# Two changes to a diffusion trunk on one core: how modulation vectors are summed and spread, and how gathers are spaced over a loop

## The chip, the cores and the metric

One Trainium2 chip, one core, one launch. The metric is the time of the whole program on the device in microseconds (us). A kernel is run several times and its median is compared. Engines are named as in the profile: PE (matrix multiply) with PEld (its weight loads), DVE (vector), ACT (scalar), POOL, and SP, which here only issues transfers.

## The reference

A two-layer trunk over 256 latent and 256 context tokens of width 1024, in float32. Cut to what matters here:

```
for l in 0, 1:
    m  = silu(c)     @ ada_w[l] + ada_b[l]      # 6 vectors of 1024 for the latent tokens
    mc = silu(c_ctx) @ ada_w[l] + ada_b[l]      # the same for the context tokens
    sh1, sc1, g1, sh2, sc2, g2 = split(m)       # v = 0 .. 5 in the kernel
    h  = rmsnorm(x, norm1_g[l]) * (1 + sc1) + sh1
    y  = mixer(h, hc)                           # attention, a different one in each layer
    x  = x + g1 * y
    h2 = rmsnorm(x, norm2_g[l]) * (1 + sc2) + sh2
    x  = x + g2 * peer_ffn(h2)                  # sum over 16 of 16384 experts per head and token
    # context tokens likewise in layer 0 only (csh1 ... cg2 from mc)
out = rmsnorm(x, final_norm_g)
```

So each layer has six modulation vectors of 1024 numbers, twice (latent, context). Shifts and scales (v = 0, 1, 3, 4) are needed with the feature on the partition; gates (v = 2, 5) are needed as a row that is the same on all 128 partitions. `peer_ffn` multiplies every token with all 16384 rows of `peer_u`, weighs, and multiplies with all rows of `peer_v`; in layer 0 the fourth block of 128 tokens takes another way: it gathers, for each of its 128 (head, choice) pairs, one row of `peer_u` and one of `peer_v` per token by index.

## The kernel before

The program runs through fixed stages: a start (the first modulation vectors and the first norm), the mixer of layer 0, the expert stage of layer 0 (`peer(0, ...)`), the mixer of layer 1, the expert stage of layer 1, a last norm. Instructions of an engine run in one order that is fixed when the kernel is built; each waits for what it reads and for the buffer that it writes.

**Modulation.** `ada_mm(l, v, half, pool)` works out 512 columns of vector v for both token kinds. The left operand `cs` is silu(c) and silu(c_ctx), padded to 32 columns, as eight tiles of 128 inputs. The right operand comes in four tiles of 512 KB (`take(("ada", ...))`), each 128 output columns with all 1024 inputs. PE is used as four column groups of 32 (`tile_position=(0, 32 * j)`): group j sums input tiles 2j and 2j+1 for all 512 columns. So the result lies in PSUM as [128, 512]: four partial sums in rows 32j and 32j+1. A DVE add (L252) takes it out and adds the bias tile `bt`, which POOL has cleared (L238) and SP has loaded two rows into (L239).

`ada_end` adds up the four partial sums and brings them into their form. For shifts and scales four small matmuls with `rt` as stationary operand and the selector `sel` (128 x 2) give features on partitions (L270); a copy (L275) or a multiply with the norm's gain (L278) writes `self.mod`. For gates a matmul with the selector `selb` as stationary operand gives a [128, 512] tile with the row on all partitions (L261), once per token kind that the layer needs (two in layer 0, one in layer 1); ACT copies it out (L262), and SP stores its 256 KB in a DRAM tensor `gb` of 128 equal rows (L263). `out_proj` (L407) and `residual` (L1245) load 512 KB of it each, with

```
g = self.m.t("g4", [128, 1024], name="gb")
nc.sync.dma_start(g, self.gb[l, 0, s])
```

There are 24 halves (2 layers, 6 vectors, 2 halves): 16 of shifts and scales, 8 of gates. They are spread as a filler, a step at a time, between other work: `ada_first` at the start (v = 0, 1 of layer 0, 4 halves), `fill` in mixer0 (v = 2, 3, 4; 6 halves), `fill` in the prologue of `peer(0)` (v = 5 of layer 0, v = 0, 1 of layer 1; 6 halves), and `fill` in mixer1 (v = 2 to 5 of layer 1; 8 halves). `bt`, `ar` and `gbo` share the buffers "a2": 3 in mixer0, 2 in the prologue and in mixer1.

**Gathers.** The main loop of `peer(0)` has 128 iterations. Iteration j multiplies chunk j of `peer_v` (`fchunk`, 18 matmuls of 512 columns for three token blocks). While j + 27 < 128, it also multiplies chunk j + 27 of `peer_u` (`achunk`, 24 matmuls of 384 columns); so iterations 0 to 100 are long and 101 to 127 short. DVE, in its order, splits the next chunks into a rounded and a rest part (L169, with ACT's L168), makes the next weights (L1176, L1178), and then uses gathered tiles: n < 128 for the dot product with u (L1143), n from 128 to 255 for the sum over v (L1148). The gather of tile n + 5 is issued by POOL when tile n has been used, five buffers in all. How many are used in an iteration is said by `pace`, from iteration 12 to 124:

```
def at(i):
    return i + min(i, NCH - lag)
return min(256, -(-256 * (at(j + 1) - at(LATE)) // (at(NCH - 3) - at(LATE))))
```

Long iterations so count twice as much as short ones: 48 long ones use three tiles and 41 use two (226), of the short ones 6 use two and 18 one (30).

Of the kernel before, what the change touches and what calls it, by code (L numbers as in the profile page):

```python
# [10 lines left out]
F = mybir.dt.float32  # L11
# [5 lines left out]
OP = mybir.AluOpType  # L17
# [5 lines left out]
NCH = 128  # L23
EPS = 1e-6
NEG = -1e30
FMIN = -3e38
LAM_INIT = 0.8 - 0.6 * math.exp(-0.3)
MLA_SCALE = 96 ** -0.5
LAG = (27, 47)
LATE = 12  # L30
# [19 lines left out]
PK = {}  # L50
_o = 0
for _n, _w in (("n1_0", 8), ("n1_1", 8), ("n2_0", 8), ("n2_1", 8), ("qn", 2), ("kvn", 1), ("sub", 1),
               ("sink", 8), ("lam", 4), ("c", 16)):
    PK[_n] = (_o, _w)
    _o += _w
PK_W = _o
CK = {}
_o = 0
for _n, _w in (("ident", 128), ("iota", 128), ("lo", 16), ("sel", 2), ("selb", 256), ("r64", 128), ("r32", 128)):
    CK[_n] = (_o, _w)  # L60
    _o += _w
CK_W = _o
# [28 lines left out]
class Kernel:  # L91
# [141 lines left out]
    def ada_mm(self, l, v, half, pool):  # L233

        nc = self.nc
        n = 2 * v + half
        bt = pool.t("a2", [128, 512], name="bt")
        nc.gpsimd.memset(bt, 0.0)  # L238
        nc.sync.dma_start(bt[0:2, :], self.A["ada_b"][l, n * 512:n * 512 + 512].partition_broadcast(2))  # L239
        p = self.ps()  # L240
        for b in range(4):
            w = self.take(("ada", l, 4 * n + b), load=ADA_LOAD)
            for q in range(2):
                for j in range(4):
                    k = 2 * j + q
                    nc.tensor.matmul(p[32 * j:32 * j + 32, b * 128:(b + 1) * 128], self.cs[:, k, :],  # L246
                                     w[:, k * 128:(k + 1) * 128], start=(q == 0), stop=(q == 1),
                                     tile_position=(0, 32 * j))
            if b % 2:
                yield None  # L250
        rt = pool.t("a2", [128, 512], name="ar")
        nc.vector.tensor_tensor(rt, p, bt, op=OP.add)  # L252
        yield rt

    def ada_end(self, l, v, half, rt, pool):
        nc = self.nc
        if v in (2, 5):
            for s in range(2 if l == 0 else 1):
                g = pool.t("a2", [128, 512], name="gbo")
                p = self.ps()  # L260
                nc.tensor.matmul(p, self.ck("selb")[:, s * 128:(s + 1) * 128], rt, start=True, stop=True)  # L261
                nc.scalar.copy(g, p)  # L262
                nc.sync.dma_start(self.gb[l, v // 3, s][:, half * 512:half * 512 + 512], g)  # L263
                yield
            return
        if half == 0:
            self.mod[l, v] = self.const([128, 8, 2], name=f"mod{l}{v}")
        p = self.ps([128, 8])
        for k in range(4):
            nc.tensor.matmul(p[:, 2 * k:2 * k + 2], rt[:, k * 128:(k + 1) * 128], self.ck("sel"),  # L270
                             start=True, stop=True)
        oh = self.mod[l, v][:, half * 4:half * 4 + 4, :]
        ph = p.rearrange("p (k s) -> p k s", s=2)
        if v in (0, 3):
            nc.vector.tensor_copy(oh, ph)  # L275
        else:
            g = self.pk("n%d_%d" % (1 if v == 1 else 2, l))[:, half * 4:half * 4 + 4]
            nc.vector.scalar_tensor_tensor(oh, ph, 1.0, g[:, :, None].to_broadcast([128, 4, 2]), op0=OP.add,  # L278
                                           op1=OP.mult)
        yield  # L280

# [115 lines left out]
    def out_proj(self, l, yh, yl, src, T):  # L397
        nc = self.nc
        gs, xs = [], []
        sq = [self.small([128, 2], "sq") for _ in range(T)]  # L400
        for t in range(T):
            x = self.m.t("q4", [128, 1024], name="x")
            nc.sync.dma_start(x, src[t])
            xs.append(x)
        for s in range(T // 2):
            g = self.m.t("g4", [128, 1024], name="gb")
            nc.sync.dma_start(g, self.gb[l, 0, s])  # L407
            gs.append(g)
        rst = []
        for half in range(2):  # L410
            c = slice(half * 512, half * 512 + 512)
            ps = [self.ps() for _ in range(T)]

            def part(t, b, wh, wl):
                tt = slice(t * 128, (t + 1) * 128)
                for q in range(2):
                    wc = slice(q * 512, q * 512 + 512)
                    self.mm3(ps[t], yh[:, 2 * b + q, tt], yl[:, 2 * b + q, tt], wh[:, wc], wl[:, wc],
                             b == 0 and q == 0, b == 3 and q == 1)

            for b in range(2):
                w = self.take(("wout%d" % l, half * 4 + b))
                for t in range(T):
                    part(t, b, *w)
            w = [self.take(("wout%d" % l, half * 4 + b)) for b in (2, 3)]
            for t in range(T):
                for b in (2, 3):
                    part(t, b, *w[b - 2])
                tmp = self.m.t("h2", [128, 512], name="yt")
                nc.vector.tensor_tensor(tmp, ps[t], gs[t // 2][:, c], op=OP.mult)  # L430
                nc.vector.tensor_tensor(xs[t][:, c], xs[t][:, c], tmp, op=OP.add)
                rs = self.squares(xs[t], half, sq[t], ps[t])
                if half:
                    rst.append(rs)
        return xs, rst
# [555 lines left out]
    def peer(self, l, xs, sq, nd):  # L991
# [203 lines left out]
        def pace(j):  # L1195

            def at(i):
                return i + min(i, NCH - lag)
            return min(256, -(-256 * (at(j + 1) - at(LATE)) // (at(NCH - 3) - at(LATE))))

        nu = 0
        load_v(0)
# [28 lines left out]
    def residual(self, l, f):  # L1231

        nc = self.nc
        T = len(f)
        sq = [self.small([128, 2], "sq") for _ in range(T)]
        self.m = Phase(self.tc, "mix%d" % (l + 1), M_BUFS[1])
        xs = []
        for t in range(T):
            x = self.m.t("q4", [128, 1024], name="x")
            nc.sync.dma_start(x, self.xd[t])  # L1240
            xs.append(x)
        gs = []
        for s in range((T + 1) // 2):
            g = self.m.t("g4", [128, 1024], name="gb")
            nc.sync.dma_start(g, self.gb[l, 1, s])  # L1245
            gs.append(g)
        rst = [None] * T
        for t in (3, 0, 1, 2) if T == 4 else range(T):
            for half in range(2):
                b = slice(half * 512, half * 512 + 512)  # L1250
                tmp = self.m.t("h2", [128, 512], name="ft")
                nc.vector.tensor_tensor(tmp, f[t][half], gs[t // 2][:, b], op=OP.mult)
                nc.vector.tensor_tensor(xs[t][:, b], xs[t][:, b], tmp, op=OP.add)
                rst[t] = self.squares(xs[t], half, sq[t], f[t][half])
            if l == 0:
                nc.sync.dma_start(self.xd[t], xs[t])
        self.pq.close()
        self.pq = Phase(self.tc, "pm%d" % (l + 1), M_PS, PSUM)
        return xs, rst

    def run(self):
# [1 line left out]
        A = self.A  # L1263
        self.mod = {}
        self.roping, self.pre = None, {}
        self.gb = self.dp.tile([2, 2, 2, 128, 1024], F, name="gb")
        self.pkt = self.const([128, PK_W], name="pk")
        self.m = Phase(self.tc, "mix0", M_BUFS[0])
        self.pq = Phase(self.tc, "pm0", M_PS, PSUM)
# [103 lines left out]
def col_blocks(w):  # L1373

    k, n = w.shape
    return np.ascontiguousarray(w.reshape(8, 128, n // 128, 128).transpose(2, 1, 0, 3)).reshape(n // 128, 128, 1024)


def row_pairs(w):

    k, n = w.shape
    return np.ascontiguousarray(w.reshape(4, 2, 128, n).transpose(0, 2, 1, 3)).reshape(4, 128, 2 * n)


def layout(x, c, ctx, c_ctx, ada_w, ada_b, norm1_g, norm2_g, w_out, peer_wq, peer_keys, peer_u, peer_v,
# [2 lines left out]
    f = np.float32  # L1388
    z = {}
    z["x"] = np.concatenate([x[0], ctx[0]], 0).reshape(4, 128, D)  # L1390
    z["ada_w"], z["ada_b"] = np.stack([col_blocks(ada_w[l]) for l in range(2)]), ada_b
    pk = np.zeros((128, PK_W), f)

    def put(n, a):
        o, w = PK[n]
        pk[:a.shape[0], o:o + w] = a

    for l in range(2):
        put("n1_%d" % l, norm1_g[l].reshape(8, 128).T)
        put("n2_%d" % l, norm2_g[l].reshape(8, 128).T)  # L1400
    put("qn", mla_q_norm_g[0].reshape(2, 128).T)
    put("kvn", mla_kv_norm_g[0].reshape(128, 1))
    put("sub", diff_subln_g[0].reshape(128, 1))
# [6 lines left out]
    def putc(n, a):  # L1410
        o, w = CK[n]
        ck[:, o:o + w] = a
# [1 line left out]
    putc("ident", np.eye(128, dtype=f))  # L1414
    putc("iota", np.broadcast_to(np.arange(128, dtype=f), (128, 128)))
    putc("lo", np.broadcast_to(np.array(CAND_LO, f), (128, 16)))
    par = np.arange(128) % 32
    putc("sel", np.stack([par == 0, par == 1], 1).astype(f))
    putc("selb", np.repeat(np.stack([par == 0, par == 1], 1).astype(f), 128, axis=1))
    putc("r64", rope_perm(64))  # L1420
    putc("r32", rope_perm(32))
    z["ck"] = ck
# [65 lines left out]
```

## Time and profile before

| | us |
|---|---|
| median of 3 runs (2666.21 to 2673.65) | 2668.47 |
| the profiled execution | 2661.32 |
| its span, first to last instruction | 2659.5 |
| PE busy in the span | 2553.3 |
| DVE busy | 1868.8 |
| ACT busy | 1201.5 |
| POOL busy | 514.6 |

The span is what the trace shows of one execution. Busy time counts an engine that has an instruction under way; consecutive matmuls overlap, so the time that one more matmul costs is the distance between starts, not its duration. The chain of waits gives that distance: each of its pieces is what the end had to wait for. Its records in this trace reach back to 1648 us. A stall is read from the wait in front of an instruction and from what released it.

### The profile page before, as it was taken

What the parts mean: (1) busy time and instruction counts of PE and PEld (TensorE: products, weight loads), DVE (VectorE), ACT (ScalarE), POOL (GpSimd) and SP (SyncE); (2) the same over time, 40 slices, a digit from 0 to 9 for tenths busy, and PEclk for the clock granted to TensorE, in tenths of its full rate; (3) what the DMA queues carried; (4) which work ended last, traced back from release to release, by engine and by line L of the source; (5) the groups of instructions that cost most, each with busy time, mean ns of one, the idle gap of its engine ahead of it and who ended that gap; (6) DMA issues with size and microseconds to landing.
All of it is one profiled execution on the core that took longest, in us unless ns stands there. A gap on an engine that the chain in (4) does not pass through costs nothing. (4 is left out here: it accounts for less than half of the span.)

```text
span 2659.5 us, 43074 instructions
## 1 busy us (share of the span) xinstructions
PE 2553.3 (96%) x16265; PEld 2232.6 (84%) x16265; DVE 1868.8 (70%) x3862; ACT 1201.5 (45%) x2201; POOL 514.6 (19%) x534
## 2 busy tenths in 40 slices
PE   7999999889999999999999997999999999999998
PEld 5866788778889999999999776767999999999986
DVE  4267689897877777777777756477997755555555
ACT  4255336785333333333333324354487444444444
POOL 0000000000155555556556531000000000000000
PEclk8999999999999999999999998999999999999999
DMA  7362325978688888988888863464479866666355
GB/s 292 102 232 102 110 90 170 290 232 275 223 325 317 308 311 305 318 305 309 311 314 289 283 215 111 141 236 137 159 230 298 319 231 212 212 209 213 125 192 182
DMA packets 240977, 614.15 MB, mean 231 GB/s; under 512 B 18384, under 2 KB 102608, under 8 KB 240768
## 3 DMA queue, kind: packets, MB, share of 16 engines
q1 hardware_dynamic: 203904, 477.17, 52.8%
q0 software_dynamic: 36864, 134.23, 14.4%
q8 instruction: 127, 2.08, 0.3%
q14 instruction: 82, 0.67, 0.1%
HBM read 558.90 MB, written 52.43 MB: 230 GB/s over the span
## 5 line engine op out<-in xcount | busy, mean ns | idle before, releaser
L168 ACT CAST ws<-w 128x1024 fp32r<-128x1024 f32 (+1 forms) x327 | 342.2, 1047 | 647.6 <-PE p L193 580.0
L169 DVE TENSOR_TENSOR ws<-w,ws 128x1024 fp32r<-128x1024 f32 (+1 forms) x327 | 397.4, 1216 | 236.9 <-ACT ws L168 236.7
L193 PE MATMUL p<-vs,w 128*128 128x512 f32 x1280 | 501.9, 393 | 9.7 <-DVE vs L169 9.7
L168 ACT CAST vs<-v 128x1024 fp32r<-128x1024 f32 x256 | 269.6, 1053 | 521.2 <-PE p L193 508.7
L192 PE MATMUL p<-vs,w 128*128 128x512 f32 x1280 | 500.0, 391 | 3.1 <-ACT w L1177 3.1
L194 PE MATMUL p<-vs,w 128*128 128x512 f32 x1280 | 501.4, 392 | 0.0
L192 PE MATMUL p<-hh,ws 128*128 128x384 f32 (+1 forms) x1304 | 459.9, 354 | 4.1 <-DVE fu L367 1.6
L194 PE MATMUL p<-hh,ws 128*128 128x384 f32 (+1 forms) x1304 | 455.1, 349 | 2.1 <-DVE ws L169 2.1
L193 PE MATMUL p<-hl,ws 128*128 128x384 f32 (+1 forms) x1304 | 455.2, 349 | 0.5 <-DVE hl L369 0.5
L169 DVE TENSOR_TENSOR vs<-v,vs 128x1024 fp32r<-128x1024 f32 x256 | 312.6, 1221 | 163.7 <-ACT vs L168 163.7
L192 PE MATMUL p<-hp,ws 128*128 128x256 f32 x1032 | 294.7, 286 | 2.4 <-ACT ws L168 2.4
L194 PE MATMUL p<-hp,ws 128*128 128x256 f32 x1032 | 291.9, 283 | 0.3 <-DVE ws L169 0.3
L193 PE MATMUL p<-hp,ws 128*128 128x256 f32 x1032 | 292.0, 283 | 0.0
L193 PEld LDWEIGHTS p<-vs,w 128*128 128x128 f32 x1280 | 241.3, 189 | 58.1 <-DVE vs L169 12.8
L194 PEld LDWEIGHTS p<-vs,w 128*128 128x128 f32 x1280 | 240.9, 188 | 53.6 <-DVE w L1178 2.5
L192 PEld LDWEIGHTS p<-vs,w 128*128 128x128 f32 x1280 | 241.4, 189 | 49.2 <-ACT w L1177 4.1
L192 PEld LDWEIGHTS p<-hh,ws 128*128 128x128 f32 x1304 | 246.6, 189 | 20.5 <-issue 2.8
L193 PEld LDWEIGHTS p<-hl,ws 128*128 128x128 f32 x1304 | 246.4, 189 | 15.5 <-DVE hl L369 0.7
L194 PEld LDWEIGHTS p<-hh,ws 128*128 128x128 f32 x1304 | 246.1, 189 | 13.4 <-DVE ws L169 2.3
L1148 DVE SCALAR_TENSOR_TENSOR acc<-gr,ga,acc 128x1024 f32<-128x1024 f32 x128 | 164.0, 1282 | 98.2 <-DMA gr<-in_v,ix 96.5
L1143 DVE SCALAR_TENSOR_TENSOR gr<-gr,hn 128x1024 f32<-128x1024 f32 x128 | 156.0, 1222 | 107.4 <-DMA gr<-in_u,ix 107.0
L312 POOL TENSOR_TENSOR rso<-rsm,mhalf 128x1 f32<-128x1 f32 x30 | 20.8, 694 | 1040.2 <-DVE rsm L310 1026.7
(273 smaller groups left out, 4001.9 us busy)
## 6 DMA issues: line engine op xcount, KB each, us to landing
w<-in_uT SPq DMA_DIRECT2D x256, 512.0 KB
v<-in_v SPq DMA_DIRECT2D x256, 512.0 KB
w<-in_ada_w SPq DMA_DIRECT2D x96, 512.0 KB
G<-stage SPq DMA_DIRECT2D x40, 1024.0 KB
g<-G SPq DMA_DIRECT2D x32, 768.0 KB
w<-in_wq SPq DMA_DIRECT2D x32, 512.0 KB
g<-G SPq DMA_DIRECT2D x32, 512.0 KB
w<-in_w_out SPq DMA_DIRECT2D x16, 512.0 KB
```

What stands on the lines that cost most here:

```text
L168: self.nc.scalar.copy(hi, raw)
L169: self.nc.vector.tensor_tensor(lo, raw, hi.bitcast(F), op=OP.subtract)
L192: m(out, lh, rh, start=start, stop=False)
L193: m(out, lh, rl, start=False, stop=False)
L194: m(out, ll, rh, start=False, stop=stop)
L312: nc.gpsimd.tensor_tensor(o, m, self.mhalf[:, :n], op=OP.pow)
L1143: nc.vector.scalar_tensor_tensor(t, t, 1.0, hn, op0=OP.mult, op1=OP.mult, accum_out=ga[:, 0, n:n + 1])
L1148: nc.vector.scalar_tensor_tensor(acc, t, ga[:, 0, n - 128:n - 127], acc, op0=OP.mult, op1=OP.add)
```

## The change

Modulation: the weights are laid out so that each of the four 512 KB tiles has two input tiles (256 inputs) for all 512 columns. Column group j of PE now sums all eight input tiles, for 128 columns of its own; the result is [128, 128] with nothing left to add up. Shifts and scales: DVE copies it out, one matmul with `sel` (128 x 8) brings it to features on partitions, DVE adds the bias from a small table `ab_l` loaded at the start with the other tables, and for scales a second instruction applies the norm's gain. Gates: `bt` is [128, 128], cleared by POOL and loaded by four small transfers; the sum is stored to DRAM by four transfers of one or two rows of 128 numbers; `gb` holds one row in place of 128, and the two loads of it read that row for all 128 partitions. Gathers: a long iteration counts 2.43 times a short one in place of twice: 53 long ones use three tiles and 36 two (231), of the short ones 1 uses two and 23 one (25). The table `selb` (128 x 256) goes.

```diff
+PACE = 1.43
-               ("sink", 8), ("lam", 4), ("c", 16)):
+               ("sink", 8), ("lam", 4), ("c", 16), ("ab_0", 48), ("ab_1", 48)):
-for ... ("sel", 2), ("selb", 256), ("r64", 128), ("r32", 128)):
+for ... ("sel", 8), ("r64", 128), ("r32", 128)):
 def ada_mm(self, l, v, half, pool):
-        bt = pool.t("a2", [128, 512], name="bt")
-        nc.gpsimd.memset(bt, 0.0)
-        nc.sync.dma_start(bt[0:2, :], self.A["ada_b"][l, n * 512:n * 512 + 512].partition_broadcast(2))
-        p = self.ps()
+        gate = v in (2, 5)
+        if gate:
+            bt = pool.t("a2", [128, 128], name="bt")
+            nc.gpsimd.memset(bt, 0.0)
+            for j in range(4):
+                o = n * 512 + j * 128
+                nc.sync.dma_start(bt[32 * j:32 * j + 2, :], self.A["ada_b"][l, o:o + 128].partition_broadcast(2))
+        p = self.ps([128, 128])
         for b in range(4):
             w = self.take(("ada", l, 4 * n + b), load=ADA_LOAD)
             for q in range(2):
+                k = 2 * b + q
                 for j in range(4):
-                    k = 2 * j + q
-                    nc.tensor.matmul(p[32 * j:32 * j + 32, b * 128:(b + 1) * 128], self.cs[:, k, :],
-                                     w[:, k * 128:(k + 1) * 128], start=(q == 0), stop=(q == 1),
-                                     tile_position=(0, 32 * j))
+                    o = q * 512 + j * 128
+                    nc.tensor.matmul(p[32 * j:32 * j + 32, :], self.cs[:, k, :], w[:, o:o + 128], start=(k == 0),
+                                     stop=(k == 7), tile_position=(0, 32 * j))
-        rt = pool.t("a2", [128, 512], name="ar")
-        nc.vector.tensor_tensor(rt, p, bt, op=OP.add)
+        rt = pool.t("a2", [128, 128], name="ar")
+        if gate:
+            nc.vector.tensor_tensor(rt, p, bt, op=OP.add)
+        else:
+            nc.vector.tensor_copy(rt, p)
 def ada_end(self, l, v, half, rt, pool):
         if v in (2, 5):
-            for s in range(2 if l == 0 else 1):
-                g = pool.t("a2", [128, 512], name="gbo")
-                p = self.ps()
-                nc.tensor.matmul(p, self.ck("selb")[:, s * 128:(s + 1) * 128], rt, start=True, stop=True)
-                nc.scalar.copy(g, p)
-                nc.sync.dma_start(self.gb[l, v // 3, s][:, half * 512:half * 512 + 512], g)
-                yield
+            for j in range(4):
+                o = half * 512 + j * 128
+                ns = 2 if l == 0 else 1
+                nc.sync.dma_start(self.gb[l, v // 3, 0:ns, o:o + 128], rt[32 * j:32 * j + ns, :])
+            yield
             return
-        for k in range(4):
-            nc.tensor.matmul(p[:, 2 * k:2 * k + 2], rt[:, k * 128:(k + 1) * 128], self.ck("sel"),
-                             start=True, stop=True)
+        nc.tensor.matmul(p, rt, self.ck("sel"), start=True, stop=True)
-        if v in (0, 3):
-            nc.vector.tensor_copy(oh, ph)
-        else:
-            nc.vector.scalar_tensor_tensor(oh, ph, 1.0, g[...], op0=OP.add, op1=OP.mult)
+        bias = self.pk("ab_%d" % l)[...].to_broadcast([128, 4, 2])
+        nc.vector.tensor_tensor(oh, ph, bias, op=OP.add)
+        if v in (1, 4):
+            nc.vector.scalar_tensor_tensor(oh, oh, 1.0, g[...], op0=OP.add, op1=OP.mult)
 out_proj, and residual with gb[l, 1, s]:
-            nc.sync.dma_start(g, self.gb[l, 0, s])
+            nc.sync.dma_start(g, self.gb[l, 0, s].partition_broadcast(128))
 peer, pace:
-                return i + min(i, NCH - lag)
-            return min(256, -(-256 * (at(j + 1) - at(LATE)) // (at(NCH - 3) - at(LATE))))
+                return i + PACE * min(i, NCH - lag)
+            return min(256, math.ceil(256 * (at(j + 1) - at(LATE)) / (at(NCH - 3) - at(LATE)) - 1e-9))
 run:
-        self.gb = self.dp.tile([2, 2, 2, 128, 1024], F, name="gb")
+        self.gb = self.dp.tile([2, 2, 2, 1024], F, name="gb")
```

## Rows read from the trace of the kernel before

**Rows 1.** The page: the engines' busy time, share of the span and instructions.

```profile
PE 2553.3 (96%) x16265; PEld 2232.6 (84%) x16265; DVE 1868.8 (70%) x3862; ACT 1201.5 (45%) x2201; POOL 514.6 (19%) x534
```

**Rows 2.** Windows by stage: length, PE, PEld, DVE, ACT, POOL busy, clock, DMA.

```profile
0.00:66.00 66.00, 49.63 (x431) 39.04 (x432) 31.62 (x65) 26.89 (x49) 5.50 (x14) 0.90 0.77 294
...
130.00:270.00 140.00, 132.01 (x1270) 92.39 (x1269) 97.44 (x336) 73.22 (x226) 2.10 (x4) 1.00 0.46 163
...
395.00:540.00 145.00, 133.77 (x1289) 120.09 (x1288) 133.17 (x431) 97.07 (x211) 2.63 (x5) 0.98 0.71 228
...
705.00:1465.00 760.00, 758.81 (x3833) 689.80 (x3832) 576.60 (x739) 265.49 (x367) 414.34 (x402) 1.00 0.87 309
1465.00:1595.00 130.00, 121.47 (x520) 97.66 (x519) 85.89 (x91) 39.28 (x54) 59.64 (x69) 0.99 0.73 248
...
1712.00:1800.00 88.00, 82.86 (x949) 51.67 (x948) 61.37 (x150) 45.91 (x122) 8.07 (x15) 1.00 0.65 229
```

**Rows 3.** The modulation's lines, whole span: instructions, ns least/median/most, first and last start.

```profile
L246 PE MATMUL p<-w,cs x1536: 269/273/423, 11.3 to 1782.2; 128*32 128x128 f32 x192
L270 PE MATMUL p<-ck,ar x128: 167/251/303, 17.4 to 1767.9; 128*128 128x2 f32 x128
L261 PE MATMUL p<-ar,ck x24: 592/594/697, 149.6 to 1789.0; 128*128 128x512 f32 x24
L252 DVE TENSOR_TENSOR ar<-p,bt x24: 671/688/702, 16.6 to 1784.9; 128x512 f32<-128x512 f32 x24
L278 DVE SCALAR_TENSOR_TENSOR mod<-p,pk x8: 155/167/167, 23.6 to 1768.5; 128x8 f32<-128x8 f32 x8
```

**Rows 4.** The chain of waits in mixer1: start, length, what (both in us).

```profile
1719.38 5.56 DMA gb<-gbo
...
1725.81 0.90 PE p L261 x2
...
1728.56 1.01 PE p L246 x32
...
1735.34 0.79 PE p L270 x8
...
1755.15 1.02 PE p L230 x8
```

**Rows 5.** PE's waits from 1465 to 1595 us: total, times, longest.

```profile
PE p L193 <- DVE vs L169: 8.5, 5, 3.3
```

**Rows 6.** DVE's groups by shape, 1465 to 1595 us: busy, mean ns, idle before.

```profile
L1148 DVE SCALAR_TENSOR_TENSOR acc<-gr,ga,acc 128x1024 f32<-128x1024 f32 x30 | 38.5, 1283 | 22.1 <-DMA gr<-in_v,ix 21.8
L169 DVE TENSOR_TENSOR vs<-v,vs 128x1024 fp32r<-128x1024 f32 x28 | 34.2, 1220 | 17.2 <-ACT vs L168 17.2
L1178 DVE TENSOR_TENSOR w<-ring,w 128x384 fp32r<-128x384 f32 x28 | 15.4, 550 | 0.0
```

**Rows 7.** The timeline: first and last of five stalls, then two undisturbed iterations.

```profile
1477.84 0.50 PE L193 MATMUL p<-vs,w 128*128 128x512 f32 x1 [1.44 <-DVE vs L169]
...
1560.56 0.49 PE L193 MATMUL p<-vs,w 128*128 128x512 f32 x1 [3.27 <-DVE vs L169]
...
1583.79 1.22 DVE L169 TENSOR_TENSOR vs<-v,vs 128x1024 fp32r<-128x1024 f32 x1 [2.39 <-ACT vs L168]
...
1587.87 1.22 DVE L169 TENSOR_TENSOR vs<-v,vs 128x1024 fp32r<-128x1024 f32 x1 [2.39 <-ACT vs L168]
```

**Rows 8.** The timeline of the start: the add of the second vector's first half.

```profile
21.73 0.69 DVE L252 TENSOR_TENSOR ar<-p,bt 128x512 f32<-128x512 f32 x1 [3.04 <-PE p L246]
```

**Rows 9.** The timeline of the end: two loads and their first use.

```profile
2641.28 0.32 SPq L1245 DMA_DIRECT2D gb<-gb  x1
2641.64 0.43 SPq L1330 DMA_DIRECT2D fg<-in_fg  x1
...
2645.03 0.69 DVE L1252 TENSOR_TENSOR ft<-p,gb 128x512 f32<-128x512 f32 x1 [0.71 <-PE p L194]
...
2652.47 1.41 DVE L1336 SCALAR_TENSOR_TENSOR o<-x,rso,fg 128x512 f32<-128x512 f32 x2 [0.44 <-POOL rso L312]
```

More of the change, by code (lines that the diff above doesn't have):

```diff
@@ L58 @@
 _o = 0
-for _n, _w in (("ident", 128), ("iota", 128), ("lo", 16), ("sel", 2), ("selb", 256), ("r64", 128), ("r32", 128)):
+for _n, _w in (("ident", 128), ("iota", 128), ("lo", 16), ("sel", 8), ("r64", 128), ("r32", 128)):
     CK[_n] = (_o, _w)
@@ L268, in ada_end @@
         p = self.ps([128, 8])
-        for k in range(4):
-            nc.tensor.matmul(p[:, 2 * k:2 * k + 2], rt[:, k * 128:(k + 1) * 128], self.ck("sel"),
-                             start=True, stop=True)
-        oh = self.mod[l, v][:, half * 4:half * 4 + 4, :]
+        nc.tensor.matmul(p, rt, self.ck("sel"), start=True, stop=True)
+        hs = slice(half * 4, half * 4 + 4)
+        oh = self.mod[l, v][:, hs, :]
         ph = p.rearrange("p (k s) -> p k s", s=2)
-        if v in (0, 3):
-            nc.vector.tensor_copy(oh, ph)
-        else:
-            g = self.pk("n%d_%d" % (1 if v == 1 else 2, l))[:, half * 4:half * 4 + 4]
-            nc.vector.scalar_tensor_tensor(oh, ph, 1.0, g[:, :, None].to_broadcast([128, 4, 2]), op0=OP.add,
+        bias = self.pk("ab_%d" % l)[:, 8 * v + half * 4:8 * v + half * 4 + 4][:, :, None].to_broadcast([128, 4, 2])
+        nc.vector.tensor_tensor(oh, ph, bias, op=OP.add)
+        if v in (1, 4):
+            g = self.pk("n%d_%d" % (1 if v == 1 else 2, l))[:, hs]
+            nc.vector.scalar_tensor_tensor(oh, oh, 1.0, g[:, :, None].to_broadcast([128, 4, 2]), op0=OP.add,
                                            op1=OP.mult)
@@ L1244, in residual @@
             g = self.m.t("g4", [128, 1024], name="gb")
-            nc.sync.dma_start(g, self.gb[l, 1, s])
+            nc.sync.dma_start(g, self.gb[l, 1, s].partition_broadcast(128))
             gs.append(g)
@@ L1390, in layout @@
     z["x"] = np.concatenate([x[0], ctx[0]], 0).reshape(4, 128, D)
-    z["ada_w"], z["ada_b"] = np.stack([col_blocks(ada_w[l]) for l in range(2)]), ada_b
+    z["ada_w"] = np.stack([np.concatenate([row_pairs(ada_w[l][:, 512 * n:512 * n + 512]) for n in range(12)], 0)
+                           for l in range(2)])
+    z["ada_b"] = ada_b
     pk = np.zeros((128, PK_W), f)
@@ L1400, in layout @@
         put("n2_%d" % l, norm2_g[l].reshape(8, 128).T)
+        put("ab_%d" % l, ada_b[l].reshape(48, 128).T)
     put("qn", mla_q_norm_g[0].reshape(2, 128).T)
@@ L1416, in layout @@
     putc("lo", np.broadcast_to(np.array(CAND_LO, f), (128, 16)))
-    par = np.arange(128) % 32
-    putc("sel", np.stack([par == 0, par == 1], 1).astype(f))
-    putc("selb", np.repeat(np.stack([par == 0, par == 1], 1).astype(f), 128, axis=1))
+    rows = np.arange(128)
+    putc("sel", np.stack([rows == 32 * j + s for j in range(4) for s in range(2)], 1).astype(f))
     putc("r64", rope_perm(64))
```

## The prediction, written before the changed kernel was built or run

> **What bounds the kernel now.** I read the page first, then windows by stage, the modulation's lines, the chain of waits, and last PE's waits and DVE's groups where PE stands still. The page [rows 1] shows PE busy for 2553.3 us of 2659.5 (96%), DVE 70%. The reader is to see that a product taken off PE's queue is worth about its spacing wherever PE is full, and that all of PE's idle time is only 106 us. The windows [rows 2] say where it lies: in the long iterations of the gathers' loop PE is busy 758.81 of 760 us, in the mixer and prologue stages that hold the modulation 92 to 94%, at the start 75%, and in the stage from 1465 to 1595 it loses 8.5 us. There the waits name one cause: five times PE waits for DVE's split of the next chunk of v, 8.5 us in all [rows 5, 7]. The chain in mixer1 [rows 4] runs through PE one short piece after another, with the modulation's own among them, and shows one stall, 5.56 us for a store of `gbo`.
>
> **Modulation on PE.** The first products (L246) stay the same in number and size: 1536 instructions [rows 3], 32 of them in 1.01 us of chain [rows 4], so 32 ns apart, four column groups beside one another. Each group still writes 128 columns in 32 rows; only which inputs it sums changes. I cost that at zero; the bound is a rival below.
>
> Gates lose their spreading product: 24 instructions of L261 [rows 3] are 12 products of two, at 0.90 us a pair in the chain [rows 4], so 10.8 us. Shifts and scales lose three of four selector products: 128 instructions of L270 are 16 groups of eight, at 0.79 us each in the chain. The one that remains streams 8 columns in place of 2 and has a pair of weight loads. It costs at least a quarter of the group, 0.20 us, and at most four of the 128-column products of L230 at their spacing (1.02 us for eight), 0.51 us. I take 0.30, nearer the row of the same tile; 16 x 0.49 = 7.8 us. Both ends give 4.5 to 9.4 us.
>
> By place: start 4 halves, 2.0 us; mixer0 4 halves and 4 gate products, 2.0 + 3.6 = 5.6; the prologue of the first expert stage the same, 5.6; mixer1 the same (one token kind, but two gates), 5.6. Of these I count the share that PE is busy there [rows 2]: start 75%, 1.5 us; mixer0 94%, 5.3; mixer1 94%, 5.3. In the prologue DVE is as busy as PE (133.2 and 133.8 of 145 us), so a shorter PE queue soon leaves DVE as what is late next: 4.5 us.
>
> Of the selector's cost one page speaks too. The Trainium skill (TensorEngine Tiling (Array Packing), Instruction Overhead) says that a matmul with one free column takes as long as one with sixty. By that the 8-column product would cost its quarter, 0.20 us, and the modulation would give 1.6 us more than by my value; no row here has an 8-column product.
>
> **Modulation on the other engines.** DVE's add of 128x512, 688 ns x 24 [rows 3], becomes one of 128x128: below 0.69 us, above the 0.167 us of the 128x8 row (L278), and I take 0.25, so 24 x 0.44 = 10.5 us less, against 8 extra small instructions of 0.17 us. The ACT copies of the gate tiles and 16 of 24 POOL clears go. None of this is added as a term: DVE and ACT have gaps in the mixers, and the start's part is inside its 1.5 us, since there the second vector is added at 21.73 us for 0.69 us after PE ended [rows 8], in front of the first norm. If DVE is the bound in the prologue, its six halves are worth 6 x 0.44 = 2.6 us, which is the low end there; 5.6 is the high end.
>
> **Transfers.** SP issues 8 more small bias loads (8 gate halves with four, not 24 with one) and 20 more stores (32, not 12). At 0.32 us an issue [rows 9] that is 9 us of SP's time. A gate half in mixer1 holds the queue 6 x 0.32 = 1.9 us longer, once its sum is ready; behind it stand the loads of weights, which go out three tiles ahead of use. This cover hides it; without it the cost is 4 x 1.6 + 4 x 1.9 = 14 us. The 16 other halves no longer put a bias load, which waits for POOL's clear, in that queue.
>
> The store's 5.56 us in the chain: DVE waited for a buffer that the store of 256 KB was still reading. At the stage's 229 GB/s [rows 2] such a store takes 1.1 us, so most of the wait is the queue of loads in front of it. The small stores stand in the same queue, but begin before a product (0.90 us) and a copy that are gone. So between 0 and 5.56 us are saved; I take 2.5, between the ends, as the row tells the queue and the size apart only by that estimate.
>
> A page speaks against even that. The Trainium skill (DMA: Bandwidth & Descriptors, Why a DMA increments its semaphore by 16 and not by 1) has a transfer spread over at most as many engines as its outer dimension allows: two rows, two engines, each of which takes its work in order. By it the small store waits out the same backlog, the 2.5 us would go, and the sum would be 23 in place of 25.5; the rows of a 128-partition store cannot show it.
>
> The gate rows are read back with one DRAM row for 128 partitions. At the end `gb` is issued at 2641.28 and used at 2645.03 without waiting for it; `fg`, which is already spread from one row, is issued at 2641.64 and used at 2652.47 without waiting [rows 9]. So the read lands in 3.75 us now and a spread one in at most 10.8: the cost lies between nothing (a gain is excluded, since PE releases the use) and 7.1 us. I take 0, as the number of rows written is the same 128. The tables at the start change by less than 80 KB, under 0.3 us at 294 GB/s [rows 2].
>
> **Gathers.** A short iteration takes PE 4.08 us when undisturbed [rows 7]. DVE needs for it a split (1.22 us), weights (0.55 us) and 1.283 us for each gathered tile [rows 6]: 3.05 us with one tile, 4.34 with two. With two, DVE is longer than PE even without a wait. Six short iterations use two tiles now, and PE stalls five times; the change leaves one such iteration. So I take off five sixths of 8.5 us, 7.1. A slow rest remains possible, because DVE also waits 22.1 us in 30 uses for the gathers themselves. The saving is between 0 and 8.5 us, and somewhat more if the stalls' slow clock goes with them.
>
> Long iterations take five more tiles: 231, not 226. With three tiles DVE needs 2 x 1.22 + 2 x 0.55 + 3 x 1.283 = 7.4 us. PE needs about 8.3 us (3833 records at 42 an iteration are 91 iterations in 760 us [rows 2]). So five more iterations run with 0.9 us to spare, as 48 do now with 1.2 us of PE idle in 760. I take 0.6 us of cost, half of that idle time again. Net 6.5 us.
>
> **Sum.** 1.5 + 5.3 + 4.5 + 5.3 + 2.5 + 6.5 = 25.6, say 25.5 us. The profiled execution took 2661.32 us, 7.15 us (0.3%) under the median of the three runs, 2668.47; the change is taken off the median: 2643 us.
>
> **Rivals.**
> - *The tail keeps its stalls* (chance 0.17). For it: 22.1 us of waits for gathers, so lateness of the tiles, not DVE's work, may be the cause. Against: the stalls number five, the two-tile iterations six. The tail gives nothing: 25.5 - 6.5 = 19 us, 2649.
> - *The modulation's products were filler* (0.14). For it: DVE as busy as PE in the prologue, and SP's longer queue in gate halves. Against: 94% of PE in both mixers, and its pieces in the chain. Of the 15.1 us of mixer0, prologue and mixer1 a third remains, and nothing of the store's 2.5: 1.5 + 5 + 6.5 = 13 us, 2655.
> - *Slower: the long iterations run dry* (0.03). Place: DVE's in-order queue. 53 of 89 long iterations use three tiles and have 0.9 us to spare; if gathers come later than that, each stalls PE by the mean of rows 5, 1.7 us: 53 x 1.7 = 90 us against the modulation's 19, so 2740. It decides from the point where DVE's 7.4 us and its wait exceed 8.3. Against: 48 such iterations cost 1.2 us today.
> - *The column groups don't run beside one another any more* (0.02), so that the change does not do what it says: eight sums in a row in one place of PSUM. At L230's 0.128 us instead of 0.032, 1536 x 0.096 = 147 us more. Against: the same place is written only every eighth instruction, as now.
> - A different order of instructions, since the build sets it anew, with up to 10 us lost somewhere else (0.08): 2653 to 2673.
>
> **How the numbers follow.** My forecast, 2643, has 0.56, and its own range is 2636 to 2650. The first two rivals lie inside the range up to 2659; the last three are mostly outside. The largest savings at once give 1.5 + 5.6 + 5.6 + 5.6 + 1.6 + 5.6 + 8.5 = 34 us, 2634; I go to 2631 for the clock. Measurement can tell 0.3%, 8 us, from no change: faster is below 2660.5. Forecast and the first two rivals hold 0.87; of the last case about half is within 0.3%, and a little of the second rival: faster 0.86, same 0.08, slower 0.06.
>
> **What would show it.** L261 gone, L270 with 32 instructions, L246 still about 1 us for 32; fewer than two PE waits for L169 between the last achunk and the loop's end; PE still over 99% busy in the long iterations; no long piece for the store of `ar` in mixer1's chain. Wrong would be: L246's spacing above 50 ns, weight loads that arrive late in gate halves, the tail's stalls with one tile an iteration, or PE waits in the long part.

## The result and the profile after

The changed kernel takes 2645.87 us (median of 6 runs, 2640.68 to 2652.64), the kernel before 2670.53 us beside it (6 runs, 2665.47 to 2676.2): ratio 0.9915 [0.9898, 0.9933]. On a second chip it took 2647.87 us, ratio 0.9927 [0.9905, 0.9949]. The prediction said 2643 us, or 0.9905 of the 2668.47 us it started from. The number held; several of the terms that add up to it did not, as the experiments show, so it held in part by luck.

The profiled execution after took 2645.51 us (span 2643.7), close to its median. That of before (2661.32) lay some 7 to 9 us under its own, so the two profiles differ by 15.8 us where the medians differ by 24.7. I therefore read stages from several kernels' profiles below, not from this pair alone.

The page after, engines' busy time, beside [rows 1]:

```profile
PE 2539.7 (96%) x16145; PEld 2223.6 (84%) x16145; DVE 1860.0 (70%) x3870; ACT 1195.9 (45%) x2189; POOL 529.4 (20%) x516
```

Exactly 120 PE instructions fewer: 24 for the gates, 96 for the selector. PE is busy for 13.6 us less and the span fell by 15.8, so 2.2 us are waiting; busy time also holds what the lower clock costs.

The same windows as [rows 2], shifted to about the same places of this trace (length, PE, PEld, DVE, ACT, POOL busy, clock, DMA):

```profile
0.00:66.00 66.00, 50.64 (x422) 38.94 (x423) 30.33 (x67) 27.55 (x50) 2.82 (x10) 1.00 0.79 298
130.00:270.00 140.00, 131.13 (x1256) 91.88 (x1255) 99.66 (x342) 74.50 (x228) 0.00 (x0) 1.00 0.45 159
387.00:532.00 145.00, 134.64 (x1312) 122.44 (x1311) 137.39 (x441) 99.35 (x218) 0.21 (x1) 0.96 0.71 234
700.00:1460.00 760.00, 755.81 (x3807) 685.86 (x3806) 577.07 (x734) 262.67 (x363) 444.47 (x408) 1.00 0.87 310
1457.00:1587.00 130.00, 120.87 (x523) 98.61 (x521) 82.07 (x92) 41.09 (x60) 58.11 (x64) 0.97 0.70 237
1703.00:1791.00 88.00, 82.13 (x885) 53.16 (x886) 60.23 (x155) 44.51 (x118) 4.96 (x11) 1.00 0.63 223
```

Three things to see. The start's clock is 1.00 where it was 0.90. In the long iterations PE lacks 4.2 us of 760, where it lacked 1.2. And the tail is not cured: 120.87 busy of 130, where it was 121.47, now at a mean clock of 0.97. Windows of fixed length don't start at the same product; the table in "Where the pacing went" cuts the loop at products.

The modulation's lines, beside [rows 3] (instructions, ns least/median/most, first and last start):

```profile
L252 PE MATMUL p<-w,cs x1536: 272/273/423, 11.6 to 1764.5; 128*32 128x128 f32 x192
...
L275 PE MATMUL p<-ck,ar x32: 175/256/383, 17.7 to 1751.1; 128*128 128x8 f32 x32
...
L260 DVE COPY ar<-p x16: 280/290/293, 16.5 to 1747.2; 128x128 f32<-128x128 f32 x16
...
L258 DVE TENSOR_TENSOR ar<-p,bt x8: 281/285/291, 143.5 to 1766.4; 128x128 f32<-128x128 f32 x8
...
L280 DVE TENSOR_TENSOR mod<-p,pk x16: 144/156/184, 18.3 to 1752.0; 128x8 f32<-128x8 f32 x16
...
L269 SPq DMA_DIRECT2D gb<-ar x32: 215/251/278, 144.5 to 1767.6; - x32
```

The main products keep number and duration; DVE's 688 ns add became 285 to 290 ns. Waits in the tail, 1452 to 1584 us, for PE and for DVE (total, times, longest):

```profile
PE p L194 <- DVE vs L170: 5.2, 2, 5.0
...
DVE acc L1153 <- DMA gr<-in_v,ix: 26.9, 21, 2.4
```

Five stalls that made 8.5 us [rows 5] are gone; one of 5.0 us is new. In mixer1's chain the 32 products still cost 1.01 us, and no piece waits for a gate store [rows 4]; one piece is a load of weights instead:

```profile
1707.65 1.01 PE p L252 x32
...
1712.94 6.10 DMA w<-in_ada_w
```

PE itself stood only 0.9 us for that load (0.60 and 0.33).

### The profile page after: what moved, and what is told of

It is laid out like the page before. It is cut to its first block, busy times and chain, and to the rows that moved or that the text cites. A ratio compares the mean times of both kernels' runs of the same rounds, so it can differ in the third digit from the quotient of the medians.

```text
span 2643.7 us, 42831 instructions
## 1 busy us (share of the span) xinstructions
PE 2539.7 (96%) x16145; PEld 2223.6 (84%) x16145; DVE 1860.0 (70%) x3870; ACT 1195.9 (45%) x2189; POOL 529.4 (20%) x516
```

## Experiments

Times beside the kernel before on the same chip, 5 to 12 runs each. "Loop" is the stretch of the profile from the first load of v to the start of the last DVE instruction that takes the fourth block's sums (`ft<-acc`); before 974.2 us, after 977.5.

| kernel | median us | ratio [95%] | loop us |
|---|---|---|---|
| modulation alone | 2650.67 | 0.9925 [0.9903, 0.9948] | 975.4 |
| pacing alone | 2667.02 | 0.9988 [0.9965, 1.0011] | 976.7 |
| gates spread by PE | 2647.91 | 0.9924 [0.9897, 0.9952] | 974.4 |
| four selectors | 2656.50 | 0.9956 [0.9934, 0.9977] | 972.9 |
| four selectors again | 2653.72 | 0.9943 [0.9922, 0.9964] | 970.5 |
| changed kernel again | 2647.87 | 0.9927 [0.9905, 0.9949] | 975.4 |
| factor 1.6 | 2641.20 | 0.9899 [0.9878, 0.9921] | 967.4 |
| factor 1.6 again | 2643.83 | 0.9919 [0.9893, 0.9945] | 966.2 |
| 1.43, last three at two | 2644.37 | 0.9913 [0.9892, 0.9934] | 969.6 |
| 1.6, three uses last | 2644.01 | 0.9899 [0.9875, 0.9923] | 975.4 |
| factor 2.0 | 2641.76 | 0.9891 [0.9868, 0.9914] | 975.6 |
| no gathers | 2630.77 | 0.9865 [0.9841, 0.9889] | 959.9 |

**Each half alone.** The changed kernel with the old pacing, and the kernel before with the new one:

```diff
-PACE = 1.43
+PACE = 1.0        # modulation alone; pacing alone: pace() of the change in the kernel before
```

> The changed kernel with long and short iterations weighed 2 to 1 again (PACE = 1.0), so the modulation's part of the change alone. By the prediction's terms the modulation gives 1.5 + 5.3 + 4.5 + 5.3 + 2.5 = 19 us and the pacing 6.5: this kernel is 19 us under the kernel before (ratio 0.993) and 6.5 us over the changed one. Rival, from the profile after, where the stage of the long and short iterations took 3.3 us more than before and not 6.5 less: the pacing gives nothing, and this kernel is as fast as the changed one or up to 3 us faster (ratio 0.990 or 0.991).

> The kernel before with the pacing of 2.43 to 1 alone. By the prediction 6.5 us under the kernel before (ratio 0.9976), with one or two PE waits for the split of v in the short iterations where there were five. Rival: no difference (0.999 to 1.002), because what stalls a short iteration is a gather that comes late, not a second tile in the same iteration; then the waits go on in iterations with one tile, or appear in the long ones.

Modulation alone is 17.9 us under the median of before, against 19.1 predicted. Pacing alone is 1.5 us, its interval on both sides of 1, against 6.5. Together that is 19.4 us, where the whole change gave 24.7 and, again, 21.6; the intervals are wide enough for the difference, and no run explains it otherwise. PE's waits in the tail of the first, then of the second:

```profile
PE p L194 <- DVE vs L170: 6.9, 7, 1.9
```

```profile
PE p L194 <- DVE vs L170: 8.5, 2, 8.2
```

With the old factor several small stalls, with the new one a single long one: the total is no smaller.

**Gates spread by PE again** (the change, with 128 equal rows made by PE as before; cut, `gb` and its two loads go back with it):

```diff
-                nc.sync.dma_start(self.gb[l, v // 3, 0:ns, o:o + 128], rt[32 * j:32 * j + ns, :])
+                for j in range(4):
+                    nc.tensor.matmul(p[:, j * 128:(j + 1) * 128],
+                                     self.ck("sel")[:, 2 * j + s:2 * j + s + 1].to_broadcast([128, 128]), rt, ...)
+                nc.scalar.copy(g, p)
+                nc.sync.dma_start(self.gb[l, v // 3, s][:, half * 512:half * 512 + 512], g)
```

> The changed kernel with its gate rows spread by PE again: four products of 128 columns for each row, with the selector's column as stationary operand, an ACT copy and a store of 256 KB, and gb of 128 equal rows. It gives back the 12 products of 0.90 us (here 8 instructions at 0.128 us, 1.0 us), the copies and the stores. By the prediction 12 x 1.0 us of PE at 92 to 94% and 2.5 us of stall in mixer1: 13 us slower than the changed kernel. Rival, that these products were filler between other waits: less than 5 us slower.

It came out 2.0 us above the changed kernel in the medians (2647.91 against 2645.87, and level with 2647.87), intervals overlapping. That looks like filler, but the edit changes a second thing: PE's waits for the modulation's weights (`w<-in_ada_w`) fall from 7.2 us to 2.1 in the prologue and from 0.9 to nothing in mixer1. So the 2.0 us are the price of products, copies and stores less what these 5.8 us were worth; three of mixer1's four gate rows do stand in this kernel's chain, at 0.89 to 1.09 us each. The price of the products alone is not shown. No store of `gbo` stood in mixer1's chain here either, so its size alone did not make the 5.56 us of [rows 4]. Only the two kernels with the old modulation show that piece; pacing alone has it at 4.55 us:

```profile
1720.89 4.55 DMA gb<-gbo
```

**Four selector products again**, twice:

```diff
-        nc.tensor.matmul(p, rt, self.ck("sel"), start=True, stop=True)
+        for k in range(4):
+            nc.tensor.matmul(p[:, 2 * k:2 * k + 2], rt, self.ck("sel")[:, 2 * k:2 * k + 2], start=True, stop=True)
```

> The changed kernel with four selector products of 2 columns in place of one of 8, in each of 16 halves; the numbers are the same. By the prediction 16 x 0.49 us = 7.8 us of PE, of which 7 us show: about 7 us slower than the changed kernel. Rival, filler: less than 2 us slower.

> The same kernel as the one with four selector products of two columns (128 small instructions in place of 32), again. Its first profile was its slowest execution, with stretches at a low granted clock in the mixers that no other kernel shows. Theory A (only the start's clock and the products themselves): start 120 to 121 us, mixer0 194 to 197, mixer1 107 to 109, and 4 to 7 us slower than the changed kernel, 0.9935 to 0.995 of the time before. Theory B (more small products make PE thin enough in the mixers too that its clock falls there): mixer0 and mixer1 again above 200 and 112 us with granted clocks of 0.6 to 0.8 in windows of them, 10 us slower, 0.995 to 0.9975.

They cost 10.6 and 7.9 us against the changed kernel's first median, 8.6 and 5.9 against its second. The dips of the clock in mixer0 and mixer1 that the first profile had were absent in the second (mixer0 194.0 us, mixer1 109.0, start 119.1), so theory A holds for that profile, with a median (0.9943) in its range and 5.9 to 7.9 us where it said 4 to 7. These products were not filler. By the code they stand between a sum and the norm or the heads that need it; that this is the reason no run shows. In the start the clock joins in (last section).

**Where the pacing went.** DVE reads its instructions in order. By the order of its instructions, the factor of 1.43 puts three uses right in front of the last two splits of the transition from long to short iterations; the old factor had three uses one split earlier. Four kernels are meant to tell that apart from late transfers (the second cut to its changed lines, the third in words):

```diff
+PACE = 1.6                                              # factor 1.6
+n1 = pace(j) if j < 98 else min(256, pace(97) + 2 * (j - 97) if j < 101 else pace(97) + j - 94)   # last three at two
         def gather / def use:  return at once            # no gathers
```

> The changed kernel once more, unedited, so that it stands beside the next three on one chip. Stage from the first load of v to the end of the loop's sums: 977.5 us in its first profile. Both theories expect 975 to 979 us again, one stall of PE of 5 to 8 us shortly after the last long iteration, and 0.990 to 0.993 of the time of the kernel before.

> The changed kernel with long iterations counted 2.6 times a short one in place of 2.43: 232 tiles in long iterations, and no short iteration with two. In DVE's order the last long iterations now read three uses, split, two uses, two splits, where the changed kernel has two uses, split, three uses, two splits. Theory A (the long stall is an accident of the order: three uses of late gathers stand directly in front of the last split that PE waits for): no PE stall over 3 us after the transition, stage 968 to 971 us, 6 to 8 us faster than the changed kernel. Theory B (at the transition the transfers come late whatever the order, since the next layer's loads and loads of v at twice the rate meet the gathers there): a stall of 4 to 8 us remains and the stage stays at 974 to 978 us, no difference that can be measured.

> The changed kernel with its factor of 1.43, but the last three long iterations use two tiles each and each later iteration one, so that the two uses left over go to the last short iterations. DVE's order at the transition: two uses, split, two uses, two splits. Theory A: no stall over 3 us, stage 968 to 971 us. Theory B: a stall of 4 to 8 us remains, 974 to 978 us.

> The changed kernel without its 256 gathers and their 256 uses (the sum of the fourth token block over the experts is left at zero). It shows what the gathers cost the loop in all. Theory A: PE runs the loop at the spacing of its products; the stage takes 977.5 less the long stall of 5 us and the small ones of 1 to 3 us, 965 to 970 us. Theory B: the loads of v and of the next layer's weights are late by themselves, so the stall after the transition stays at 3 us or more, 972 us or more.

The changed kernel showed its stall again (5.19 us at 1472.16). DVE in its tail, then with the factor of 1.6 (start, duration, shape, idle before):

```profile
1460.13 1.28 DVE L1153 SCALAR_TENSOR_TENSOR acc<-gr,ga,acc 128x1024 f32<-128x1024 f32 x1 [1.58 <-DMA gr<-in_v,ix]
1461.34 1.22 DVE L170 TENSOR_TENSOR vs<-v,vs 128x1024 fp32r<-128x1024 f32 x1
...
1464.61 1.29 DVE L1153 SCALAR_TENSOR_TENSOR acc<-gr,ga,acc 128x1024 f32<-128x1024 f32 x1 [0.71 <-DMA gr<-in_v,ix]
...
1467.64 1.28 DVE L1153 SCALAR_TENSOR_TENSOR acc<-gr,ga,acc 128x1024 f32<-128x1024 f32 x1 [1.29 <-DMA gr<-in_v,ix]
1471.21 1.28 DVE L1153 SCALAR_TENSOR_TENSOR acc<-gr,ga,acc 128x1024 f32<-128x1024 f32 x1 [2.28 <-DMA gr<-in_v,ix]
1472.41 1.22 DVE L170 TENSOR_TENSOR vs<-v,vs 128x1024 fp32r<-128x1024 f32 x1
...
1473.69 0.79 PE L194 MATMUL p<-vs,w 128*128 128x512 f32 x1 [4.99 <-DVE vs L170]
```

```profile
1459.42 2.60 DVE L1153 SCALAR_TENSOR_TENSOR acc<-gr,ga,acc 128x1024 f32<-128x1024 f32 x2
1461.93 1.22 DVE L170 TENSOR_TENSOR vs<-v,vs 128x1024 fp32r<-128x1024 f32 x1
...
1464.83 1.28 DVE L1153 SCALAR_TENSOR_TENSOR acc<-gr,ga,acc 128x1024 f32<-128x1024 f32 x1 [0.34 <-DMA gr<-in_v,ix]
...
1466.50 1.28 DVE L1153 SCALAR_TENSOR_TENSOR acc<-gr,ga,acc 128x1024 f32<-128x1024 f32 x1
1467.70 1.22 DVE L170 TENSOR_TENSOR vs<-v,vs 128x1024 fp32r<-128x1024 f32 x1
...
1468.97 0.50 PE L194 MATMUL p<-vs,w 128*128 128x512 f32 x1 [1.14 <-DVE vs L170]
```

In the first, three waits (4.28 us) and three uses stand between two splits that were 11.07 us apart; in the second there are two uses, one wait of 0.34, and 5.77 us. Factor 1.6 had PE waits of 0.89 and 1.14 us in the tail, the capped kernel 0.2 in all. Their loops are 10.1 and 7.9 us shorter than the changed kernel's first, 8.0 and 5.8 than its second. In these two traces the gathers with the stall are not clearly slower, they are issued later: POOL issued the three at 1459.41, 1460.66 and 1462.55 us, from 1.9 us before the first split to 1.2 after it, and they were used 5.2, 7.0 and 8.7 us after their issue; the two of the factor 1.6 were issued 5.1 and 3.8 us before the first split and used 8.0 and 8.4 us later. Without gathers the loop takes 959.9 us: they cost 14.3 us before, 17.6 after, 7.5 with the factor of 1.6.

**The reversal.** From the factor of 1.6, one use moved one iteration later:

```diff
-                n1 = pace(j)
+                n1 = pace(j) - (j == 99)
```

> The kernel with the factor of 1.6, with one use moved: iteration 99 uses two tiles in place of three and iteration 100 three in place of two. In DVE's order nothing else moves: two uses, split, three uses, two splits, as in the changed kernel, where the factor of 1.6 alone had three uses, split, two uses, two splits. Theory A (the order in front of the last two splits makes the long stall): a stall of 4 to 8 us is back about 16 us after the last long iteration, with low granted clock behind it; stage 973 to 977 us, 5 to 9 us slower than with the factor alone. Theory B (the factor itself, by fewer tiles left for the short iterations, made the difference): no stall over 2 us, 966 to 969 us.

> The changed kernel with a factor of 2.0 (long iterations count three times a short one): 235 tiles in long iterations, 57 of them with three. The order at the transition is that of the factor of 1.6. Theory A: short iterations have still more room, long ones have some left; stage 964 to 969 us, same as with 1.6 within 3 us. Theory B (the prediction's slower rival: with three tiles the long iterations run dry): PE waits for splits in the long part add up to over 10 us, stage above 978 us.

> The kernel with the factor of 1.6 once more, since one profile of each order is little: the changed kernel and three others with three uses in front of the last two splits each showed a stall of 4.5 to 8.2 us there, and the kernel with the factor of 1.6 has one profile without it. Theory A (the order): again no stall over 2 us after the last long iteration, stage 966 to 970 us, 0.988 to 0.991 of the time before. Theory B (the first profile was a lucky one, transfers come late in some executions whatever the order): a stall over 4 us, 973 us or more.

The stall came back, in DVE and PE of that kernel:

```profile
1467.88 1.28 DVE L1153 SCALAR_TENSOR_TENSOR acc<-gr,ga,acc 128x1024 f32<-128x1024 f32 x1 [6.96 <-DMA gr<-in_v,ix]
...
1472.07 1.22 DVE L170 TENSOR_TENSOR vs<-v,vs 128x1024 fp32r<-128x1024 f32 x1
...
1473.34 0.80 PE L194 MATMUL p<-vs,w 128*128 128x512 f32 x1 [7.33 <-DVE vs L170]
```

Loop 975.4 us, 8.0 more than with the factor alone. The repeat of the factor 1.6 had none again (0.72 and 1.18 us, loop 966.2). Over all profiles: seven with three uses in front of those splits (the changed kernel twice, pacing alone, gates by PE, four selectors twice, the reversal) stalled 4.5 to 8.2 us there; four with another order and a factor over 1 (1.6 twice, capped, 2.0) at most 1.65 us. That is theory A, with one limit: timed, the reversal is only 0.2 to 2.8 us slower than the two medians of factor 1.6, its interval overlaps theirs, and their medians lie 5 to 9 us above their profiled executions. Those, and that of the capped kernel, are the fastest executions of their kernels. So the order goes with the stall in the profiles; how much time it costs over many executions is not shown, and executions without a profile may stall in either order. The order needs a late gather to do harm; why one lands late (6.96 us here, 10.3 us after its issue at 1457.57 us) stays open.

The factor of 2.0 has no long stall (1.65 and 0.70 us), but its loop of 975.6 us misses theory A, and theory B's waits are missed too: those over 0.3 us from 702 to 1465 us make 5.4 us, not 10. Its long part:

```profile
705.00:1465.00 760.00, 755.32 (x3798) 684.34 (x3797) 581.67 (x741) 262.48 (x363) 441.51 (x411) 1.00 0.88 312
```

Cut at products, the loops compare better. The long part goes from the first product of chunk 12 of v, about where the uses begin, to the last product with u; the tail goes from there to the loop's end (us, one profile each):

| kernel | long part | tail |
|---|---|---|
| before | 732.5 | 128.0 |
| modulation alone | 734.5 | 125.6 |
| pacing alone | 733.8 | 127.2 |
| changed kernel, again | 738.7, 734.4 | 123.2, 125.4 |
| factor 1.6, again | 731.8, 732.7 | 118.4, 118.2 |
| 1.6, three uses last | 734.0 | 125.4 |
| 1.43, last three at two | 734.1 | 115.9 |
| factor 2.0 | 738.8 | 118.4 |
| no gathers | 730.8 | 115.0 |

What the tail saves with 57 groups of three (9.6 us against before), the long part gives back in good part (6.3). The factor of 1.6 keeps it. The changed kernel's two profiles differ by 4.3 us in the long part, so one profile is weak evidence for a few us.

The best versions of the runs are those of 1.6 and 2.0, 2641 to 2644 us; pooled, factor 1.6 is 2642.3 (median of 12 runs) and the changed kernel 2646.9 (12 runs), not on one chip throughout.

## Why the prediction came out right, and where it did not

Stage by stage, from eleven profiles: "old" is the mean of the two kernels with the old modulation, "new" that of the nine with the change's modulation whole, least to most in brackets (us). Pacing does not touch these stages.

| stage | old | new | gain | predicted |
|---|---|---|---|---|
| start, to the last rotation product | 119.4 | 116.1 (115.5 to 117.1) | 3.2 | 1.5 |
| mixer0 | 195.5 | 193.5 (191.3 to 195.8) | 2.0 | 5.3 |
| prologue | 305.9 | 298.2 (297.4 to 298.9) | 7.7 | 4.5 |
| mixer1, to its last sums | 109.6 | 105.3 (104.5 to 106.2) | 4.3 | 7.8 |
| the modulation | | | 17.2 | 19.1 |

- **Main products: right.** 1536, 1.01 us for 32; the column groups kept their concurrency.
- **Selector: right in kind, taken too small.** From its first product to the next one's start, a group of eight and the two instructions that replace it, in the prologue before and after:

```profile
505.98 0.95 PE L270 MATMUL p<-ck,ar 128*128 128x2 f32 x8
506.79 1.08 PE L973 MATMUL p<-og,oh 128*128 128x128 f16 x16
```

```profile
487.29 0.34 PE L275 MATMUL p<-ck,ar 128*128 128x8 f32 x2
487.48 0.52 PE L231 MATMUL p<-ck,ijg 128*128 128x128 f32 x3
```

  That is 0.81 us and 0.19; in mixer1 0.88 and 0.22, against 0.30 taken. By the Trainium skill (TensorEngine Tiling (Array Packing), Instruction Overhead) a half would have cost its quarter, estimated at 0.20 us; these rows agree, and so do the medians of the durations (251 ns with 2 columns [rows 3], 256 with 8). In the start a half is dearer, 0.37 us (last section) and more. Over all sixteen the distance falls from 14.5 to 4.9 us, by 9.6 where 7.8 were counted. Put back, the three others cost 6 to 11 us timed.
- **Small transfers: put at nothing, not free.** "This cover hides it", and weight loads that arrive late were a sign of being wrong. PE's waits for them over the span, before and after:

```profile
PE p L246 <- DMA w<-in_ada_w: 15.7, 9, 8.0
```

```profile
PE p L252 <- DMA w<-in_ada_w: 18.4, 11, 8.0
```

  In the prologue they rose from 4.8 us to 7.2 (6.9 to 7.4 in the nine), in mixer1 from nothing to 0.9 (0.4 to 1.0). Whether the small transfers in front of the loads do it, or the halves that now follow one another sooner, was not tried.
- **Gates' products: not settled.** 10.8 us were taken at nearly full price; put back, with 5.8 us less waiting for weights, they cost about 2 net. The second rival, filler with SP's longer queue, gets its outcome here in part and is wrong for the selector.
- **Mixer0: high by 3.3.** Neither half of the modulation put back shows there (193.4 with the gates, 194.0 with the second profile of the selectors), within a spread of 4.5 us.
- **Store's stall: gone, worth little.** It is in the chain of both kernels with the old modulation and in none with the new. But in the kernel before PE stood only 1.44 us for the sum behind it (1725.81 us), and mixer1 gained 4.3 us in all: 109.0 in the second profile with four selectors leaves 3.7 of these to the selectors, and some 0.6 us for gate products and stall together, not 2.5 + 3.6 x 0.94. After, the next gate add (1710.48 us) had no wait behind stores issued from 1705.33 on. Whether a store of two rows waits out a backlog, as the prediction concluded from the Trainium skill (DMA: Bandwidth & Descriptors, Why a DMA increments its semaphore by 16 and not by 1), no run here shows; the stores of mixer1, where it applied this, hold one row each, since layer 1 has one token kind.
- **Start: low by 1.7.** Part of it is the clock, which the prediction gave only to the range (last section).
- **Prologue: low by 3.2, not settled.** Putting back gates costs it 1.4 us, selectors 0.3 to 1.3; 5 us or more of its 7.7 no run explains. The prediction's high end (5.6) with DVE's 2.6 us added would be near it, but I had set these against each other, and DVE's add, the bias load and POOL's clear were not tried alone.
- **Gathers: the step that failed.** "I take off five sixths of 8.5 us", against 0.6 of cost in the long iterations. Against before, the tail became 4.8 and 2.6 us shorter in the two profiles of the changed kernel and 0.8 with pacing alone, not 7.1; the long part became 6.2, 1.9 and 1.3 us longer. Net that is 1.4 us worse, 0.7 better and 0.5 worse. The whole loops are 3.3, 1.2 and 2.5 us longer, but the other 2 us lie in the first twelve iterations, which use no tile. Timed, pacing is 1.5 us better alone [0.9965, 1.0011]. The small stalls did go, as the count of two-tile short iterations says, but the moved uses made one long stall at the transition. With another order the tail did give more than 7.1: 9.6 and 9.8 us with the factor of 1.6. The first rival said the outcome (2649 us); its reason, waits for tiles, is 4.28 us of the 11.07 between the two splits.
- **The slower rivals did not occur.** Even with 57 three-tile iterations the long part was 6.3 us longer than before, not 90.

So 2643 stood 3 to 5 us under 2645.87 and 2647.87: the modulation gave about what was counted, with errors of both signs inside it that happened to cancel, and the pacing some 5 us less by its run alone.

## What to carry over

Put a removed product back to price it, and look what else the edit moves: the selectors were worth their full spacing, and behind the gates' 2 us net 5.8 us of waits for weights had moved the other way. When work is moved between iterations, write out the in-order queue at the place where the kinds of iteration meet; one use before or after a split went with a stall of 7 us there in the profile, and with 0.2 to 2.8 us in the medians. Compare stages over several profiles before crediting one: mixer0 alone spread by 4.5 us between kernels that are the same there.

## What the chip showed that was not expected

The start holds two halves' selector products back to back. Before, then after (start, duration, shape):

```profile
37.67 1.08 PE L246 MATMUL p<-w,cs 128*32 128x128 f32 x32
38.68 1.99 PE L270 MATMUL p<-ck,ar 128*128 128x2 f32 x16
40.53 1.07 PE L230 MATMUL p<-ck,xn 128*128 128x128 f32 x8
43.00 1.22 PE L192 MATMUL p<-hh,ws 128*128 128x512 f32 x2 [1.40 <-ACT hh L365]
44.02 1.91 PE L230 MATMUL p<-ck,xn 128*128 128x128 f32 x8
```

```profile
38.03 1.08 PE L252 MATMUL p<-w,cs 128*32 128x128 f32 x32
39.04 0.87 PE L275 MATMUL p<-ck,ar 128*128 128x8 f32 x4
39.77 1.07 PE L231 MATMUL p<-ck,xn 128*128 128x128 f32 x8
42.24 0.73 PE L193 MATMUL p<-hh,ws 128*128 128x512 f32 x2 [1.40 <-ACT hh L370]
42.91 1.08 PE L231 MATMUL p<-ck,xn 128*128 128x128 f32 x8
```

Both then stand 1.40 us. Before, the eight transposes at 44.02 us last 1.91 us, after 1.08. The granted clock from 40 to 49 us, before, after, and with four selectors again:

```profile
40.00:49.00 9.00, 7.60 (x33) 6.34 (x33) 6.16 (x13) 4.18 (x8) 0.84 (x2) 0.62 0.80 307
```

```profile
40.00:49.00 9.00, 7.60 (x41) 5.99 (x40) 6.59 (x14) 4.09 (x8) 0.18 (x1) 1.00 0.73 253
```

```profile
40.00:49.00 9.00, 7.60 (x41) 6.48 (x41) 6.01 (x14) 4.19 (x8) 0.20 (x1) 0.81 0.72 273
```

All four profiles with 16 small products there fell to the lower level (1.2 GHz) for part of this stretch, 0.62 to 0.81 on average; of the ten with four products one did (0.81, without gathers) and nine stayed at 1.00. So the term of 1.5 us became 3.2. How much of that is the clock one profile tells: the kernel without gathers, with four products and 0.81, needed 117.1 us for the start, 1.1 over the mean of the other eight. The long stall in the tail has the same after-effect: behind its 4.99 us the clock from 1472 to 1478 us was 0.50 in the changed kernel, 1.00 with the factor of 1.6:

```profile
1472.00:1478.00 6.00, 4.31 (x10) 3.36 (x11) 4.90 (x6) 0.00 (x0) 0.00 (x0) 0.50 0.75 233
```

```profile
1472.00:1478.00 6.00, 6.00 (x29) 4.95 (x28) 2.52 (x4) 2.19 (x3) 3.38 (x5) 1.00 0.76 224
```

The five short stalls before left the tail at a mean clock of 0.99 [rows 2]. In time both tails lost more than the stalls' length: against the tail without gathers (115.0 us), the one before took 13.0 us more, with 8.5 us of stalls, and the changed kernel's 8.2, with 5.2.
